# A layer kernel on one core: elementwise work of the mixer moved from GpSimd to VectorE, the tail's second factor and its half sums treated otherwise, and a new order list

## The chip, the cores and the metric

The kernel runs on one core of one Trainium2 chip. The metric is the device time of an execution in microseconds (us). The kernel before has a median of 1092.29 us over three timed runs (1090.87 to 1093.38). A difference of 0.2% is about 2.2 us here.

The engines are named as the profile names them: PE is TensorE (matmuls; PEld is its loading of weights), DVE is VectorE, ACT is ScalarE, POOL is GpSimd, SP is SyncE, which here only issues DMAs.

## The reference

One decoder layer over 512 tokens of width 1024, in float32. Two SwiGLU layers stand around a mixer, and a gated embedding follows. What the change touches is the second half of the mixer and the last norm.

```python
def swiglu(x, w_gate, w_up, w_down):
    return (jax.nn.silu(x @ w_gate) * (x @ w_up)) @ w_down

# mixer: proj = rmsnorm(h) @ w_in, split into u, v, z, xbc, dt_raw
ya = chunked_spatial_gating(gelu(u), gelu(v), ...)            # layernorm of v, product per head, * u
# Mamba-2 half, 2 groups of 8 heads of width 64, 4 chunks of 128 tokens:
xs, bm, cm = split(silu(causal_depthwise_conv(xbc)))
xdt = xs * dt
states = einsum(bm, xdt * decay_states)                       # per chunk
y = y_diag + y_off + xs * d_skip
y = y * silu(z)
y = y * rsqrt(mean(y * y, per group) + EPS) * norm_g
h = h + concatenate([rmsnorm(ya), y]) @ w_out

# tail
gate = sigmoid(rmsnorm(h) @ ple_w_gate + ple_b_gate)
h = h + gate * (p @ ple_w_proj)
return rmsnorm(h, final_norm)                                 # h * rsqrt(mean(h * h) + EPS) * g
```

## The kernel before, in words

Activations lie feature-major: eight tiles of 128 features by 512 tokens (`h`). Every matrix product is made of fp32r matmuls in three passes: a weight tile and an activation are each split into a rounded part and a rest (`whi`, `wlo`; `xhi`, `xlo`), and high*high, high*rest and rest*high are added in PSUM. Each weight tile of 128x1024 that arrives by DMA (`raw`, `rawb`, `rawd`, `r`) so costs one ACT copy (`whi<-raw`) and one DVE subtraction (`wlo<-raw,whi`).

The two SwiGLU layers and the mixer's products with `w_z`, `w_v`, `w_u` use a seven-product scheme on 2x2 blocks (`Group`, `Quads`). Some of its weight sums are made by DMAs that add into a tile; POOL issues these (`nc.gpsimd.dma_start(..., accum_op=ALU.add)`), SP issues the plain loads.

The program records all its operations, cuts them into numbered units, and issues the units in the order of a list, `ORDER`. Each engine then runs its own instructions strictly in that order, and semaphores hold an instruction back until its inputs are there. All of these instructions carry the line of the one place that issues them (L1896), so the profile is read by tile names.

The mixer, in the order of the program: the first projections and the causal convolution (`conv`: a DVE product `convin`, an ACT start, three DVE steps of 511, 510 and 509 columns into the tile `m` that becomes `xs[n]`, an ACT Silu); for each of the two groups of heads `gates(g)` (z by `Quads`), `ssd(g)` and `gated(g)`; then `values`, `spatial`, `outer`, `mix` for the other half, and the output product.

- `ssd(g)`: PE turns four `xs` tiles chunk by chunk (`b<-ident,m`), DVE multiplies by dt (`m<-b,dt`), POOL multiplies three of the four by the decay to the chunk's end (`m<-m,toend`), PE makes the states. Then for each of 8 heads ACT builds a decay tile `u`, DVE multiplies it (`u<-u,m`), and PE makes the products with `u`; DVE adds up `y` (`m<-m,vec,b` and `m<-m,m` of 384 columns).
- `gated(g)`: POOL multiplies four `xs` tiles by z (`m<-m,m` of 512 columns), ACT squares them, POOL adds the squares up (`ssum<-ssum,tmp`, three per group), PE sums over partitions (`b<-ones,ssum`), and DVE makes the factor and scales (`m<-m,vec,rall`).

The tail: the last three of the eight gate products are cut into two halves of 256 tokens. DVE adds each half's squares to `total` (the tile `ssum` of 512 columns); `factors` sums over partitions on PE and takes the root: for the first half by `rsqrt`, which is nine small DVE steps after two that start it, for the second by `rsqrt_by_table`, an ACT Sqrt with five small DVE steps. `rows_out` turns the eight `h` tiles (`b<-ident,h`), scales (`o<-b,rlast`, one tile in two on ACT, the other on DVE) and writes out.

Of the kernel before, what the change touches and what calls it, by code (L numbers as in the profile page):

```python
# [29 lines left out]
P = 128  # L30
T = 512
NC = T // P
D = 1024
# [43 lines left out]
for _name, _w in _VECS:  # L77
# [211 lines left out]
def layer_kernel(ctx: ExitStack, tc: tile.TileContext, a: dict, out: bass.AP):  # L289
# [1210 lines left out]
    def by_head(t):  # L1500
        return t.rearrange("p (h d) -> p h d", d=HD)

    group_norm = [Norm(), Norm()]
    yb = []

    def ssd(g):
# [82 lines left out]
    def gated(g, z):  # L1589
        for m in range(4):  # L1590
            y = xs[4 * g + m]
            nc.gpsimd.tensor_tensor(y, y, z[m], ALU.mult)
            group_norm[g].add(y)
# [410 lines left out]
```

## Time and profile before

| | before |
|---|---|
| median of three runs | 1092.29 us |
| profiled execution | 1095.35 us, of it the span from first to last instruction 1093.6 us |
| PE busy | 1072.8 us (98%), 7063 matmuls |
| DVE busy | 812.5 us (74%) |
| ACT busy | 550.8 us (50%) |
| POOL busy | 127.9 us (12%), 126 instructions |
| granted PE clock, mean | 0.994 |

A busy PE is not a PE at its peak, and the shares are means over stages with different limits. In rows of the timeline the first number is the start in us from the span's start, the second the duration in us; square brackets give the idle time of the engine before it and what ended it. In grouped rows stand the count, the busy time in us, the mean duration in ns, and the idle time before them. In rows by stage each engine has its busy us and its count of instructions; then come the granted clock of PE and the share of time that the DMA engines were busy.

### The profile page before, as it was taken

The page shows a single profiled execution, that of the slowest core. Times are in us where ns is not written, and L with a number is a line of the kernel's source. Part 1 is how long each engine was busy: PE and PEld are TensorE (multiplying, and loading weights), DVE is VectorE, ACT ScalarE, POOL GpSimd, SP SyncE. Part 2 cuts the span into 40 slices and gives each one's busy share as a digit, 9 for nine tenths or more (in the row PEclk, how much of TensorE's full clock was granted, in tenths as well). Part 3 has the DMA queues.
Part 4 walks back from the last instruction along what each step waited for, and adds up shares of the span by engine and source line. Part 5 has one row for each costly group of instructions (what it writes and reads, how often), then busy time and mean ns, then how long its engine had stood idle before and what let it go on. Part 6 is the DMA issues. An engine that isn't in the chain of part 4 may idle for free.

```text
span 1093.6 us, 17428 instructions
## 1 busy us (share of the span) xinstructions
PE 1072.8 (98%) x7063; PEld 966.2 (88%) x7063; DVE 812.5 (74%) x1139; ACT 550.8 (50%) x772; POOL 127.9 (12%) x126
## 2 busy tenths in 40 slices
PE   9999999999999999988999999999999999999996
PEld 7899999999998878887999878899999899999886
DVE  6887675757667789989989765778666675767748
ACT  7654353344345448767665434454444353443536
POOL 1100000000000400152610000000000000000110
PEclk9999999999999999989999999999999999999998
DMA  8968664775632344755766333667675665643412
GB/s 315 245 176 229 174 174 149 211 157 177 174 96 67 108 129 131 183 124 149 176 165 154 93 108 116 190 132 217 194 196 135 193 182 162 161 109 116 156 57 77
DMA packets 51633, 171.16 MB, mean 157 GB/s; under 512 B 5857, under 2 KB 6113, under 8 KB 51553
## 3 DMA queue, kind: packets, MB, share of 16 engines
q1 hardware_dynamic: 34128, 117.46, 31.4%
q0 software_dynamic: 11824, 43.00, 21.8%
q10 hardware_dynamic: 5600, 9.60, 2.8%
q8 instruction: 55, 0.90, 0.4%
q14 instruction: 26, 0.21, 0.1%
HBM read 165.77 MB, written 4.26 MB: 155 GB/s over the span
## 4 chain that ended last, share of the span: by engine, by line
PE 89%; DVE 5%; DMA 2%; issue 2%; ACT 1%; POOL 1%; DVEq 0%; SPq 0%; POOLq 0%; ACTq 0%
PE b L1896 73%; PE a L1896 16%; DVE m L1896 2%; DMA r<-in_w_z 2%; DVE wlo L1896 1%; DVE u L1896 1%; POOL m L1896 0%; DVE r L1896 0%; DMA g<-in_p 0%; ACT whi L1896 0%; ACT m L1896 0%; ACT L1896 0%; DVE tmp L1896 0%; POOL ssum L1896 0%; ACT u L1896 0%
## 5 line engine op out<-in xcount | busy, mean ns | idle before, releaser
L1896 PE MATMUL b<-xfb,whi 128*128 128x256 f32 (+1 forms) x1648 | 291.0, 280 | 0.0
L1896 PEld LDWEIGHTS b<-xfb,whi 128*128 128x128 f32 x1648 | 253.1, 188 | 6.9 <-issue 1.0
L1896 PE MATMUL b<-xfb,wlo 128*128 128x256 f32 (+1 forms) x824 | 230.7, 280 | 0.0
L1896 DVE TENSOR_TENSOR wlo<-raw,whi 128x1024 fp32r<-128x1024 f32 (+1 forms) x127 | 160.1, 1265 | 62.1 <-ACT whi L1896 60.0
L1896 ACT CAST whi<-raw 128x1024 fp32r<-128x1024 f32 (+1 forms) x128 | 133.2, 1042 | 124.6 <-PE b L1896 97.0
L1896 PEld LDWEIGHTS b<-xfb,wlo 128*128 128x128 f32 x824 | 154.7, 188 | 1.1
L1896 PE MATMUL b<-xfa,whi 128*128 128x256 f32 (+1 forms) x688 | 126.2, 285 | 0.0
L1896 PEld LDWEIGHTS b<-xfa,whi 128*128 128x128 f32 x688 | 106.4, 188 | 3.5
L1896 PE MATMUL b<-xfa,wlo 128*128 128x256 f32 (+1 forms) x344 | 98.1, 285 | 0.0
L1896 ACT CAST whix<-rawd 128x1024 fp32r<-128x1024 f32 (+1 forms) x40 | 39.5, 987 | 108.4 <-PE a L1896 58.4
L1896 ACT CAST whi<-rawb 128x1024 fp32r<-128x1024 f32 x52 | 54.6, 1049 | 65.8 <-PE b L1896 48.7
L1896 DVE TENSOR_TENSOR wlox<-rawd,whix 128x1024 fp32r<-128x1024 f32 (+1 forms) x40 | 45.6, 1141 | 43.5 <-ACT whix L1896 43.5
L1896 POOL DMA_DIRECT2D raw<-in_ffn_gu x30 | 33.2, 1125 | 360.1 <-DVE wlo L1896 165.6
L1896 DVE TENSOR_TENSOR wlo<-rawb,whi 128x1024 fp32r<-128x1024 f32 x52 | 63.5, 1221 | 13.9 <-ACT whi L1896 13.8
L1896 PE MATMUL b<-m,whi 128*128 128x512 f32 x224 | 70.7, 396 | 0.0
L1896 PEld LDWEIGHTS b<-xfa,wlo 128*128 128x128 f32 x344 | 64.6, 188 | 1.0
L1896 PE MATMUL b<-xb,whi 128*128 128x256 f32 (+1 forms) x280 | 63.4, 322 | 0.1
L1896 PE MATMUL b<-ghi,wlox 128*128 128x512 f32 x156 | 61.5, 394 | 0.0
L1896 PE MATMUL b<-glo,whix 128*128 128x512 f32 x156 | 61.3, 393 | 0.0
L1896 PE MATMUL b<-ghi,whix 128*128 128x512 f32 x156 | 60.7, 389 | 0.0
L1896 PE MATMUL a<-ghi,wlox 128*128 128x512 f32 x140 | 55.2, 394 | 0.0
L1896 PE MATMUL a<-glo,whix 128*128 128x512 f32 x140 | 54.9, 392 | 0.0
(295 smaller groups left out, 2305.7 us busy)
## 6 DMA issues: line engine op xcount, KB each, us to landing
raw<-in_ffn_gu SPq DMA_DIRECT2D x56, 512.0 KB, 5.4
rawd<-in_ffn_down SPq DMA_DIRECT2D x40, 512.0 KB, 5.2
rawb<-in_ffn_gu SPq DMA_DIRECT2D x32, 512.0 KB, 6.7
raw<-in_ffn_gu POOLq DMA_DIRECT2D x30, 512.0 KB, 7.9
s<-in_ffn_gu SPq DMA_DIRECT2D x20, 512.0 KB, 5.3
s<-in_ffn_gu POOLq DMA_DIRECT2D x20, 512.0 KB, 8.1
raw<-in_w_out SPq DMA_DIRECT2D x16, 512.0 KB, 3.7
raw<-in_w_in SPq DMA_DIRECT2D x13, 512.0 KB, 3.7
```

The source lines that it names most:

```text
L1896: getattr(getattr(real, engine), what)(*(real_of(x) for x in args), **{k: real_of(x) for k, x in kw.items()})
```

## The change

Five edits and a new list:

1. `group_norm = [Norm(), Norm()]` becomes `[Norm(nc.vector), Norm(nc.vector)]`: the three additions of squares per group, 128x512, go from POOL to DVE.
2. In `ssd`, the product with `to_end` (three per group, 128x512) goes from POOL to DVE.
3. In `gated`, the product with z (four per group, 128x512) goes from POOL to DVE. With these, 20 instructions of 128x512 move.
4. In the tail, the additions of the squares of the second and third last product (two per half, 128x256) go from DVE to POOL.
5. The first half's factor is taken by `rsqrt_by_table` too.
6. `ORDER` is made anew, in its first 240 units and from the middle of the mixer's first projections to the end of the output product, and in the last units.

```diff
@@ ssd, gated, and their norms
-    group_norm = [Norm(), Norm()]
+    group_norm = [Norm(nc.vector), Norm(nc.vector)]
...
                 xd = whole_m()
-                nc.gpsimd.tensor_tensor(by_head(xd), by_head(t), heads(to_end, g, c), ALU.mult)
+                nc.vector.tensor_tensor(by_head(xd), by_head(t), heads(to_end, g, c), ALU.mult)
...
             y = xs[4 * g + m]
-            nc.gpsimd.tensor_tensor(y, y, z[m], ALU.mult)
+            nc.vector.tensor_tensor(y, y, z[m], ALU.mult)
             group_norm[g].add(y)
@@ the tail: gate_half, factors
         if d < ND - 1:
-            nc.vector.tensor_tensor(total[:, tok], total[:, tok], sq, ALU.add)
+            nc.gpsimd.tensor_tensor(total[:, tok], total[:, tok], sq, ALU.add)
...
-        (rsqrt_by_table if tok.start else rsqrt)(rt, ps[:, :2], 1.0 / D, (P, 2))
+        rsqrt_by_table(rt, ps[:, :2], 1.0 / D, (P, 2))
@@ ORDER: one line of the list
-    "823 825 787 872 836 882 801-802 837 803 935 873 943 838 890 936 883 804 944-945 839-840 1015 841 805 "
+    "787 801-802 872 935 837 873 943 838 890 816 944 839-840 817 841-844 882 818 845-847 945 803 819 891 "
```

The list moves instructions at many places; three are shown.

**POOL, around `gated` of the second group.** Before (`m<-m,m` is the product with z, `ssum` the sum of squares, the DMAs add weight blocks):

```order
L1896 DMA raw_4984<-in_w_v 128x1024
L1896 TENSOR_TENSOR m_3773<-m_3773,m_4973 128x512
L1896 TENSOR_TENSOR m_3781<-m_3781,m_5157 128x512
L1896 TENSOR_TENSOR m_3776<-m_3776,m_5143 128x512
L1896 TENSOR_TENSOR m_4705<-m_4705,m_5160 128x512
L1896 TENSOR_TENSOR ssum_5306<-ssum_5306,tmp_5310 128x512
L1896 TENSOR_TENSOR ssum_5306<-ssum_5306,tmp_5322 128x512
L1896 TENSOR_TENSOR ssum_5306<-ssum_5306,tmp_5320 128x512
L1896 DMA r_797_5407<-in_w_v 128x1024
```

And after the change:

```order
L1896 DMA r_715_4861<-in_w_v 128x1024
L1896 DMA raw_5043<-in_w_v 128x1024
L1896 DMA r_787_5375<-in_w_v 128x1024
L1896 DMA raw_5379<-in_w_u 128x1024
L1896 DMA r_788_5377<-in_w_v 128x1024
```

Between the weight DMAs of the mixer POOL has no product and no sum left; two masks (`AFFINE_SELECT`) of the spatial part stay on it.

**DVE, ahead of the second group's turning.** The tile `m` whose three convolution steps (511, 510, 509) end last is the last one that PE turns. Before, the steps stand directly ahead of the first product with dt, which reads what PE turned:

```order
L1896 SCALAR_TENSOR_TENSOR m_4705<-convin_4585,vec_63,m_4705 128x511
L1896 TENSOR_TENSOR m_3774<-m_3774,m_3770 128x384
L1896 TENSOR_SCALAR nrt_121<-rtok_112 128x4
L1896 TENSOR_TENSOR wlo_4819<-r_662_4450,whi_4802 128x1024
L1896 TENSOR_TENSOR wlo_4821<-r_683_4607,whi_4806 128x1024
L1896 SCALAR_TENSOR_TENSOR m_4705<-convin_4585,vec_63,m_4705 128x510
L1896 SCALAR_TENSOR_TENSOR m_4705<-convin_4585,vec_63,m_4705 128x509
L1896 TENSOR_TENSOR wlo_4873<-raw_4611,whi_4812 128x1024
L1896 TENSOR_TENSOR m_4951<-b_4875,dt_122 128x512
```

After the change the last step of that convolution stands 37 rows ahead of that product; around the product:

```order
L1896 TENSOR_TENSOR r_663_4451<-r_663_4451,r_690_4638 128x1024
L1896 TENSOR_TENSOR wlo_4786<-r_690_4638,whi_4770 128x1024
L1896 TENSOR_TENSOR m_3870<-m_3870,m_3868 128x384
L1896 TENSOR_TENSOR wlo_4789<-r_663_4451,whi_4782 128x1024
L1896 TENSOR_TENSOR m_3870<-m_3870,m_4622 128x512
L1896 TENSOR_TENSOR m_3872<-m_3872,m_4540 128x512
L1896 TENSOR_TENSOR wlo_4890<-raw_4644,whi_4866 128x1024
L1896 TENSOR_TENSOR m_4892<-b_4793,dt_122 128x512
```

The two 512-column products with z (`m_3870`, `m_3872`), which were POOL's, stand there among the splits of weights.

**ACT, the tail.** `tmp<-tmp,vec` is a Sigmoid, `tmp<-h` a Square, `h<-h,vec` the last gain, `ny<-nv` the Sqrt. Before:

```order
L1896 ACTIVATE tmp_10758<-tmp_10758,vec_63 128x256
L1896 ACTIVATE h_96<-h_96,vec_63 128x512
L1896 ACTIVATE tmp_10771<-h_98 128x256
L1896 ACTIVATE h_98<-h_98,vec_63 128x256
L1896 ACTIVATE tmp_10774<-h_97 128x256
L1896 ACTIVATE h_97<-h_97,vec_63 128x256
L1896 ACTIVATE o_10427<-b_10800,rlast_141 128x512
L1896 ACT_TABLE_LOAD
L1896 ACTIVATE ny_10831<-nv_10826 128x2
```

After:

```order
L1896 ACTIVATE tmp_10762<-tmp_10762,vec_63 128x256
L1896 ACT_TABLE_LOAD
L1896 ACTIVATE ny_10769<-nv_10764 128x2
L1896 ACTIVATE tmp_10776<-h_95 128x256
L1896 ACTIVATE tmp_10778<-h_96 128x256
L1896 ACTIVATE o_10413<-b_10798,rlast_141 128x512
L1896 ACTIVATE o_10414<-b_10788,rlast_141 128x512
L1896 ACTIVATE h_95<-h_95,vec_63 128x256
L1896 ACTIVATE ny_10826<-nv_10821 128x2
```

The table load now stands ahead of the second half's two squares, and no load stands ahead of the second root.

233 rows, old and new, of the table ORDER are left out of this document.

## The prediction

> **What bounds the kernel now.** I read the page first, then PE's waits, then the mixer by stage.
>
> ```profile
> span 1093.6 us, 17428 instructions
> PE 1072.8 (98%) x7063; PEld 966.2 (88%) x7063; DVE 812.5 (74%) x1139; ACT 550.8 (50%) x772; POOL 127.9 (12%) x126
> ```
>
> PE is busy for all but 20.8 us of the span, and the change takes nothing off PE: its matmuls stay. So the time can fall only by idle PE time, by time at a lowered clock, and by what stands after the last matmuls. PE's waits in order of size:
>
> ```profile
> PE b L1896 <- ACT m L1896: 3.1, 1, 3.1
> PE b L1896 <- DVE m L1896: 2.1, 2, 1.1
> PE b L1896 <- DVE u L1896: 2.0, 2, 1.7
> ...
> PE b L1896 <- DVE ssum L1896: 1.3, 1, 1.3
> PE a L1896 <- DVE tmp L1896: 1.1, 1, 1.1
> PE a L1896 <- ACT a L1896: 0.7, 1, 0.7
> PE b L1896 <- DVE wlo L1896: 0.7, 1, 0.7
> PE a L1896 <- DVE wlo L1896: 0.7, 1, 0.7
> ```
>
> The columns are total, count, longest. The wait for `ssum` is the tail's; the other seven rows, 10.4 us in nine waits, lie in the mixer between 445 and 570 us. By stage:
>
> ```profile
> 10.00:45.00 35.00, 35.00 (x170) 28.93 (x169) 30.81 (x50) 23.66 (x35) 4.68 (x7) 1.00 0.91 307
> 427.00:532.00 105.00, 95.84 (x743) 87.43 (x741) 98.16 (x135) 77.69 (x143) 36.13 (x28) 0.97 0.64 162
> 483.00:491.00 8.00, 7.99 (x42) 8.00 (x43) 5.36 (x15) 4.88 (x14) 0.00 (x0) 0.57 0.63 149
> ```
>
> After the length stand PE, PEld, DVE, ACT, POOL, the granted clock, the DMA share. From 427 to 532 DVE is busy for 98.2 of 105 us, more than PE: there DVE sets the pace. And the third row shows a second loss, a granted clock of 0.57 over 8 us: 8 × 0.43 = 3.4 us of PE's work. It stands directly behind the largest gap:
>
> ```profile
> 478.80 3.43 DVE L1896 SCALAR_TENSOR_TENSOR m<-convin,vec,m 128x510 f32<-128x510 f32 x2
> 482.32 0.63 ACT L1896 ACTIVATE m<-m 128x512 f32<-128x512 f32 x1 [3.80 <-DVE m L1896]
> 483.01 1.39 PE L1896 MATMUL b<-ident,m 128*128 128x128 f32 x8 [3.12 <-ACT m L1896]
> ```
>
> PE's wait is put down to ACT's Silu, but ACT itself had waited 3.80 us for DVE: the last two convolution steps end late.
>
> **Why DVE is so full: POOL beside it.** The same instructions in the mixer's busy stretch (440 to 537 us), by form:
>
> ```profile
> L1896 DVE TENSOR_TENSOR wlo<-r,whi 128x1024 fp32r<-128x1024 f32 x14 | 20.9, 1496 | 0.3 <-ACT whi L1896 0.3
> L1896 DVE TENSOR_TENSOR u<-u,m 128x512 f32<-128x512 f32 x16 | 14.2, 909 | 0.0
> L1896 DVE TENSOR_TENSOR wlo<-raw,whi 128x1024 fp32r<-128x1024 f32 x5 | 9.9, 1987 | 0.0
> ...
> L1896 DVE TENSOR_TENSOR m<-m,m 128x384 f32<-128x384 f32 x8 | 5.8, 730 | 0.0
> L1896 DVE TENSOR_TENSOR m<-m,b 128x384 f32<-128x384 f32 x8 | 4.4, 550 | 0.0
> ...
> L1896 DVE SCALAR_TENSOR_TENSOR m<-convin,vec,m 128x511 f32<-128x511 f32 x2 | 2.5, 1262 | 0.0
> L1896 DVE SCALAR_TENSOR_TENSOR m<-convin,vec,m 128x510 f32<-128x510 f32 x2 | 2.5, 1254 | 0.0
> L1896 DVE SCALAR_TENSOR_TENSOR m<-convin,vec,m 128x509 f32<-128x509 f32 x2 | 2.4, 1186 | 0.0
> ```
>
> and behind the mixer, 580 to 700 us, where POOL computes nothing:
>
> ```profile
> L1896 DVE TENSOR_TENSOR wlo<-raw,whi 128x1024 fp32r<-128x1024 f32 x20 | 24.3, 1220 | 13.3 <-ACT whi L1896 11.3 <-PE b L1896 2.0
> ...
> L1896 DVE SCALAR_TENSOR_TENSOR m<-m,vec,rall 128x512 f32<-128x512 f32 x10 | 6.9, 744 | 0.0
> ...
> L1896 DVE TENSOR_TENSOR m<-m,tmp 128x512 f32<-128x512 f32 x8 | 5.4, 686 | 0.1
> ```
>
> The excess: 14 × (1496 − 1220) = 3.9; 16 × (909 − 686) = 3.6; 5 × (1987 − 1220) = 3.8; 8 × (730 − 550) = 1.4; the six convolution steps 2 × (1262 + 1254 + 1186 − 3 × 744) = 2.9. Together 15.6 us. The 384-column pair points at the cause: `m<-m,b`, with its second operand in PSUM, takes 550 ns, `m<-m,m`, both in SBUF, 730. What POOL does in the mixer:
>
> ```profile
> L1896 POOL TENSOR_TENSOR m<-m,m 128x512 f32<-128x512 f32 x8 | 14.9, 1883 | 6.7 <-DVE m L1896 4.1 <-ACT m L1896 2.1 <-issue 0.5
> L1896 POOL TENSOR_TENSOR ssum<-ssum,tmp 128x512 f32<-128x512 f32 x6 | 10.7, 1781 | 0.2
> L1896 POOL TENSOR_TENSOR m<-m,toend 128x512 f32<-128x512 f32 x6 | 6.8, 1318 | 1.6 <-DVE m L1896 1.6
> L1896 POOL DMA_DIRECT2D r<-in_w_z x4 | 3.5, 880 | 48.2 <-DVE wlo L1896 34.5 <-PE b L1896 13.8
> ```
>
> 20 instructions, 32.4 us. The Trainium skill ("GPSIMD Engine Reference", section "1. Specifications") says that GpSimd's path to SBUF is shared with VectorE, and that they contend where VectorE's instruction reads two inputs from SBUF; the 384-column pair (730 against 550 ns) agrees.
>
> **The change: the mixer.** *Added on DVE:* the 20 instructions. Such a one takes 0.68 us, and in a full queue the next begins after 0.60:
>
> ```profile
> 1071.43 0.68 DVE L1896 TENSOR_TENSOR h<-h,tmp 128x512 f32<-128x512 f32 x1
> 1072.03 0.68 DVE L1896 TENSOR_TENSOR tmp<-tmp,emb 128x512 f32<-128x512 f32 x1
> ```
>
> 20 × 0.60 = +12.0 us. *Relieved:* between 0 (the excess has another cause) and −15.6. I take −15.6, because the whole excess sits in instructions with two inputs in SBUF. DVE's balance there is −3.6 us. That is small; what counts is which waits end.
>
> *The 3.1 us gap.* In the new order the last convolution ends 37 DVE rows ahead of the product that reads its turned tile, so neither Silu nor turning is late: −3.1, and with it the 3.4 us at half clock behind it. The bounds for the clock are 0 (halved again behind another gap) and −3.4. I take −3.4, since the remaining gaps, of 1.7 us or less, left the clock whole everywhere else in the mixer: the mean of 0.97 over 105 us is those 3.4 us.
>
> *The 1.1 us gap* for `tmp` ends with its cause, DVE's wait for POOL's last sum:
>
> ```profile
> 531.74 0.69 DVE L1896 TENSOR_TENSOR tmp<-a,m 128x512 f32<-128x512 f32 x1 [1.18 <-POOL ssum L1896]
> ```
>
> On DVE the sum costs 0.60, counted above, and stands in DVE's own order: −1.1.
>
> *Given back.* A product with z on DVE now waits for the Silu of z with splits queued behind it; on POOL that was 2.1 us in all, seen in its row. So new waits cost between 0 and 2.1. I take +0.9, the mean of the seven mixer waits left (10.4 − 4.2 = 6.2 us). Mixer: −3.1 − 3.4 − 1.1 + 0.9 = **−6.7**. It fits DVE: 98.2 − 3.6 = 94.6 of 105 − 6.7 = 98.3 us is 96% busy, so little more can come. POOL's weight DMAs gain nothing from an empty POOL: they waited 34.5 us for `wlo`, a buffer still in use.
>
> **The change: the tail.**
>
> ```profile
> 1085.51 0.16 DVE L1896 TENSOR_SCALAR nv<-b 128x2 f32<-128x2 f32 x1
> ```
> ```profile
> 1081.23 0.71 ACT L1896 ACTIVATE h<-h,vec 128x512 f32<-128x512 f32 x1
> ...
> 1082.28 0.51 ACT L1896 ACTIVATE h<-h,vec 128x256 f32<-128x256 f32 x1
> ...
> 1085.24 1.28 ACT L1896 ACT_TABLE_LOAD   x1
> 1086.54 0.20 ACT L1896 ACTIVATE ny<-nv 128x2 f32<-128x2 f32 x1
> ```
>
> Before, the second root stood ready at 1085.67 and waited for the load until 1086.54: −0.87. Now load and first root (1.28 + 0.20) stand ahead of the second half's last squares, but two gains leave that place (0.71 + 0.51), so the squares end some 0.3 later. Then two sums on POOL replace two on DVE, there 0.34 each by half of the 512-column row of 0.68. No row has POOL at 256 columns; half of the means of its 512-column rows gives 0.66 to 0.94. One behind the other they cost 0.6 to 1.2 more. If the first runs under the next square, and since POOL's queue is empty where DVE's held the factor's steps between the sums, it may cost as little as nothing. Tail: −0.9 + 0.3 + (0 to 1.2) = −0.6 to +0.6. I take −0.3, nearer the low end, because the first sum needs only the first of the two squares. The new list's first 240 units I cost at 0 ± 0.3: from 10 to 45 us PE is busy without a break (first stage row), which covers a different order of splits there.
>
> The Trainium skill ("ScalarE: Activation LUTs", section "What ACT_TABLE_LOAD costs") adds a drain of 1.38 us to each load. By it the load ahead of the squares would make the tail 1.4 us worse, +1.1 in place of −0.3, and the sum 1086.7, still within the forecast's range. The trace disagrees: the load is one row of 1.28 us, and the root started 0.02 us after its end.
>
> **Sum.** −6.7 − 0.3 = −7.0. The profiled execution took 1095.35 us, 1.75 around its span; it would take 1088.3. It stood 3.1 over the median of the runs, so on their scale 1092.3 − 7.0 = **1085.3 us**.
>
> **Rivals.**
>
> *More.* Every mixer gap closes: −10.4 − 3.4 − 0.3 = −14.1, about 1078; with half of the rest, 1081.5, where I draw the line. For it: each remaining wait but one names DVE, and DVE gets faster. Against: DVE stays 96% busy. Chance 0.10.
>
> *No change.* The gaps only move. The accumulating DMAs take long beside a full DVE:
>
> ```profile
> 435.07 7.05 DMA r<-in_w_z
> ```
>
> If the new list puts the first use of such a transfer 4 us behind its issue, PE waits 3 us, the clock halves again behind that, and 3.1 + 3.4 come back: −0.5, about 1091.8. Against: the 14 splits that read `r` had only 0.3 us of idle time ahead of them (their row above). Chance 0.13.
>
> *Slower: DVE becomes the bound.* If the excess isn't POOL's but comes from DMA traffic, DVE must do 98.2 + 12.0 = 110.2 us in a stretch of 105: +5.2, about 1097.5. It decides if the relief falls below 12.0 − 6.8 = 5.2 of the 15.6 us (6.8 is DVE's idle time there). For it: DMAs are busy for 0.64 of these stages, and no run yet shows DVE there without POOL. Against: the 384-column pair, 730 and 550 ns, ran in the same stages beside the same transfers, and only the one with both operands in SBUF is slow; traffic alone would have to pick that one out too. Chance 0.15. The order leaves no doubt that POOL's mixer products are gone.
>
> **Numbers.** A measurement of this kernel tells 0.2%, 2.2 us, from no change, so faster begins at 1090.1. The forecast (1081.5 to 1090.1) has 0.62: its own terms (clock 0 to −3.4, new waits 0 to 2.1, tail and start to their ends) give 1083.8 to 1091.1. Faster: 0.62 + 0.10 = 0.72; same 0.13; slower 0.15. The range, 1079.5 to 1093.0, leaves out the slower case and the far end of "more".
>
> **What would show it.** The splits back at 1220 ns, `u<-u,m` at 686, and no DVE row near 2 us: the relief is POOL's. No halved stretch in the mixer, mean clock above 0.997, no PE wait for `ACT m` of 3 us: the large term holds. No DVE wait for POOL's `ssum` near 530 us; DVE's total near 812.5 − 3.6 = 809, a little below for the tail's four sums. In the tail: Sqrt directly behind its `nv`, and PE's wait for POOL's `ssum` near 1.3 us. Wrong is the forecast if `wlo` stays above 1.35 us without POOL, or if a new gap of 3 us or more appears; then the list, not the engine, decides.

## The result and the profile after

The change makes the kernel faster by more than was forecast: 1080.07 us (1079.39 to 1081.09, four runs) against 1092.84 us (1090.87 to 1095.73) for the kernel before. The ratio is 0.9882, its 95% interval 0.9858 to 0.9906, which is 10.3 to 15.5 us. The forecast was 1085.3 us with a range of 1079.5 to 1093.0. The measured time is in that range by 0.6 us only, and 1.4 us beyond the 1081.5 where the prediction drew the line to its rival "more".

The page of the kernel after, its first lines:

```profile
span 1077.7 us, 17409 instructions
PE 1067.5 (99%) x7063; PEld 962.3 (89%) x7063; DVE 803.8 (75%) x1149; ACT 550.1 (51%) x773; POOL 96.6 (9%) x110
```

PE now idles for 1077.7 − 1067.5 = 10.2 us of the span, where it was 20.8. The span is 15.9 us shorter: 10.6 of idle time, and 5.3 by which PE's own busy time shrank. (The medians differ by 12.8: the profiled execution of before stood 2.5 us over its median, that of after 0.7 under.)

The split of a weight tile that both kernels do near the end, and a sum that both do ahead of the mixer, show where the time went. The timeline of DVE, first before, then after:

```profile
342.32 0.68 DVE L1896 SCALAR_TENSOR_TENSOR h<-b,h 128x512 f32<-128x512 f32 x1
...
1058.26 1.23 DVE L1896 TENSOR_TENSOR wlo<-raw,whi 128x1024 fp32r<-128x1024 f32 x1 [0.19 <-ACT whi L1896]
```
```profile
341.87 0.68 DVE L1896 SCALAR_TENSOR_TENSOR h<-b,h 128x512 f32<-128x512 f32 x1
...
1041.39 1.23 DVE L1896 TENSOR_TENSOR wlo<-raw,whi 128x1024 fp32r<-128x1024 f32 x1 [0.19 <-ACT whi L1896]
```

Ahead of the mixer the kernel after is 0.4 us earlier, behind it 16.9: the stretch between gave 16.4, and since PE is busy without a break from 570 to 1040 us in both, that is the mixer. From that split to the end of the span it was 35.3 us and is now 36.3: the tail lost 1.0.

PE's waits after, all of them from 0.3 us up (total, count, longest):

```profile
PE b L1896 <- DVE tmp L1896: 1.7, 1, 1.7
PE b L1896 <- DVE h L1896: 1.2, 1, 1.2
PE b L1896 <- ACT whi L1896: 0.7, 1, 0.7
PE b L1896 <- ACT h L1896: 0.6, 1, 0.6
PE a L1896 <- ACT m L1896: 0.3, 1, 0.3
```

Only the last row lies in the mixer. The first and the third are the program's start, the two for `h` the tail. Of nine waits in the mixer, 10.4 us, one of 0.3 us is left. The stages of after, in the columns of the stage rows of before:

```profile
427.00:532.00 105.00, 105.00 (x877) 98.20 (x876) 101.36 (x160) 85.90 (x156) 11.53 (x14) 1.00 0.73 185
483.00:491.00 8.00, 8.00 (x68) 7.07 (x67) 7.47 (x22) 5.34 (x10) 0.00 (x0) 1.00 0.73 206
```

PE does not stand still once in these 105 us, the clock is whole, and DVE is fuller than before: 101.4 us, 97%. What DVE's instructions take there (425 to 520 us, by form):

```profile
L1896 DVE TENSOR_TENSOR wlo<-r,whi 128x1024 fp32r<-128x1024 f32 x15 | 18.3, 1218 | 0.8 <-ACT whi L1896 0.8
L1896 DVE TENSOR_TENSOR u<-u,m 128x512 f32<-128x512 f32 x16 | 10.8, 682 | 0.0
L1896 DVE TENSOR_TENSOR wlo<-raw,whi 128x1024 fp32r<-128x1024 f32 x7 | 8.5, 1214 | 0.0
...
L1896 DVE TENSOR_TENSOR m<-m,m 128x384 f32<-128x384 f32 x7 | 3.7, 548 | 0.0
```

1496, 909, 1987 and 730 ns have become 1218, 682, 1214 and 548, and the convolution steps take 740 ns in place of 1186 to 1262: the excess of 15.6 us is gone.

### The profile page after: what moved, and what is told of

The parts are those of the page before. It is cut to its first block, busy times and chain, and to the rows that moved or that the text cites. A ratio compares the mean times of both kernels' runs of the same rounds, so it can differ in the third digit from the quotient of the medians.

```text
span 1077.7 us, 17409 instructions
## 1 busy us (share of the span) xinstructions
PE 1067.5 (99%) x7063; PEld 962.3 (89%) x7063; DVE 803.8 (75%) x1149; ACT 550.1 (51%) x773; POOL 96.6 (9%) x110
## 4 chain that ended last, share of the span: by engine, by line
PE 98%; DVE 0%; ACT 0%; DMA 0%; issue 0%; DVEq 0%; SPq 0%; ACTq 0%
PE b L1896 80%; PE a L1896 18%; DMA raw<-in_ple_proj 0%; DVE o L1896 0%; ACT L1896 0%; DVE tmp L1896 0%; ACT tmp L1896 0%; DVE nt L1896 0%; ACT h L1896 0%; DVEq L1999 0%; ACT whi L1896 0%; ACT m L1896 0%; ACT ny L1896 0%; SPq L1896 0%; DVE h L1896 0%
## 5 line engine op out<-in xcount | busy, mean ns | idle before, releaser
L1896 DVE TENSOR_TENSOR wlo<-raw,whi 128x1024 fp32r<-128x1024 f32 (+1 forms) x127 | 155.2, 1228 | 51.2 <-ACT whi L1896 49.5
```

The costliest lines, as they stand in the source:

```text
L1896: getattr(getattr(real, engine), what)(*(real_of(x) for x in args), **{k: real_of(x) for k, x in kw.items()})
```

## The experiments

Three theories stood against each other. **A, sharing:** DVE's instructions with two operands in SBUF are slowed by POOL's work beside them, and with that gone DVE keeps up. **B, the list:** the new order is what closes the gaps. **C, POOL's queue:** results and DMA issues come late because they are queued behind other work on POOL. The kernel before, timed beside them, had medians of 1093.95 us (beside the first four kernels), 1093.58 (the second four) and 1094.31 (the last four).

| kernel | us | ratio to before, interval |
|---|---|---|
| moves, old list (`moves_old_list`) | 1091.06 | 0.9974 [0.9961, 0.9986] |
| new list, work on POOL (`new_list_pool`) | 1095.98 | 1.0018 [1.0007, 1.0030] |
| after, tail of before (`new_mixer_old_tail`) | 1079.76 | 0.9874 [0.9859, 0.9889] |
| after, 20 products more on DVE (`dve_fill`) | 1084.14 | 0.9916 [0.9901, 0.9931] |
| after, 36 products more on POOL (`pool_fill`) | 1089.39 | 0.9957 [0.9943, 0.9971] |
| `new_list_pool`, POOL's queue reordered (`pool_reordered`) | 1089.91 | 0.9965 [0.9946, 0.9985] |
| `moves_old_list`, three places mended (`moves_three_places`) | 1092.06 | 0.9984 [0.9972, 0.9996] |
| old list, the work on neither (`left_out_old_list`) | 1083.58 | 0.9904 [0.9888, 0.9920] |
| after, early table load (`early_load`) | 1078.57 | 0.9862 [0.9841, 0.9882] |
| after, half sums on DVE (`tail_sums_dve`) | 1079.84 | 0.9871 [0.9851, 0.9891] |
| after, again (`after_again`) | 1079.85 | 0.9870 [0.9846, 0.9893] |
| after, six sums on POOL (`sums_on_pool`) | 1089.77 | 0.9960 [0.9945, 0.9975] |

### Moves without the list, list without the moves

```diff
 the kernel before, ORDER unchanged (moves_old_list)
+    group_norm = [Norm(nc.vector), Norm(nc.vector)]
+                nc.vector.tensor_tensor(by_head(xd), by_head(t), heads(to_end, g, c), ALU.mult)
+            nc.vector.tensor_tensor(y, y, z[m], ALU.mult)
 the kernel after, ORDER unchanged (new_list_pool): the same three lines back to
+    group_norm = [Norm(), Norm()]; nc.gpsimd.tensor_tensor(...) in both
```

> The kernel before, with its own list and its own tail; only the 20 products and sums of the mixer go from GpSimd to VectorE. Theory A, the engine: what closes PE's gaps is that VectorE's instructions with two SBUF operands no longer share with GpSimd (15.6 us of excess gone for 12.0 us added). Then most of the gain is here too: 1081 to 1085 us against 1092 to 1093 before, the wait of PE for ACT m near 480 us falls from 3.1 to below 1 us, and wlo is back at 1.22 us. Theory B, the list: the old order still puts the last convolution directly ahead of the turning, and the moved products now stand in VectorE's queue at places chosen for another engine: 1088 to 1093 us, with a gap of 2 us or more left near 480 us though wlo is at 1.22 us.

> The changed kernel with its new list and new tail; only the 20 products and sums of the mixer go back to GpSimd. Theory A, the engine: VectorE gets the excess of about 15.6 us back and loses 12.0 us of work; with 101.4 of 105 us busy in the changed kernel it would be at 105 of 105, so waits come back: 1086 to 1092 us, wlo up to 2.3 us again. Theory B, the list: the earlier convolution and the work ahead hold even so: 1080 to 1084 us, with wlo slow but no gap over 1 us.

Neither half does it: 2.9 us faster with the moves alone, 2.0 slower with the list alone, 12.8 to 14.5 faster with both. Theory A's range for the moves (1081 to 1085 us) is missed, and both theories' ranges for the list alone. With the moves and the old list, PE's waits of 0.7 us and more, and then the stage, read:

```profile
PE b L1896 <- DVE tmp L1896: 3.9, 2, 2.3
PE b L1896 <- DVE m L1896: 2.0, 2, 1.5
PE a L1896 <- DVE tmp L1896: 1.6, 1, 1.6
PE b L1896 <- DVE ssum L1896: 1.3, 1, 1.3
PE a L1896 <- DVE wlo L1896: 1.0, 3, 0.4
PE a L1896 <- ACT a L1896: 0.7, 1, 0.7
```
```profile
427.00:532.00 105.00, 97.68 (x781) 89.65 (x780) 99.37 (x162) 79.32 (x144) 9.56 (x11) 0.98 0.66 170
```

The wait for `ACT m` has gone without any new order: with POOL's work gone from beside them, the convolution steps end early enough (0.2 us is left of 3.1). But other waits have come in its place, of 2.3, 1.5 and 1.6 us. For 97.7 us in which PE was busy DVE was busy for 99.4 here, 1.02 to one; in the kernel after it is 101.4 for 105.0, 0.97.

With the new list and the work on POOL, PE's two longest waits and the stage are others:

```profile
PE a L1896 <- ACT a L1896: 4.6, 1, 4.6
PE b L1896 <- POOL m L1896: 4.1, 1, 4.1
```
```profile
427.00:532.00 105.00, 99.95 (x801) 92.48 (x800) 90.46 (x135) 80.25 (x146) 36.00 (x28) 0.97 0.65 168
```

Over the stage DVE is not short of time, 90.5 of 105 us, where theory A expected 105: A's reason does not hold. Nor does sharing cost here what it cost before: `wlo<-r` takes 1410 ns and `wlo<-raw` 1575 (430 to 540 us), `u<-u,m` stays at 683. POOL's timeline shows the cause, with a row of DVE's behind it:

```profile
479.41 4.13 POOL L1896 TENSOR_TENSOR ssum<-ssum,tmp 128x512 f32<-128x512 f32 x2
483.51 1.05 POOL L1896 TENSOR_TENSOR m<-m,toend 128x512 f32<-128x512 f32 x1
...
521.42 5.24 POOL L1896 TENSOR_TENSOR m<-m,m 128x512 f32<-128x512 f32 x3 [8.89 <-DVE m L1896]
...
533.19 0.86 POOL L1896 DMA_DIRECT2D r<-in_w_v  x1
```
```profile
538.67 1.23 DVE L1896 TENSOR_TENSOR r<-r,r 128x1024 f32<-128x1024 f32 x1 [7.62 <-DMA r<-in_w_v]
```

The product with `to_end`, for which PE waits 4.1 us, stands behind two sums. And the DMA that adds a weight block is issued at 533.19, behind products and sums; DVE then waits 7.6 us for it and PE 4.6.

### POOL's queue

```diff
 POOL's order, new_list_pool -> pool_reordered
+L1896 TENSOR_TENSOR m_4894<-m_4892,toend_130 128x512
 L1896 TENSOR_TENSOR ssum_4870<-ssum_4870,tmp_4872 128x512
+L1896 TENSOR_TENSOR m_4899<-m_4897,toend_130 128x512
 L1896 TENSOR_TENSOR ssum_4870<-ssum_4870,tmp_4875 128x512
...
+L1896 DMA r_787_5375<-in_w_v 128x1024
+L1896 DMA raw_5379<-in_w_u 128x1024
 L1896 TENSOR_TENSOR ssum_5390<-ssum_5390,tmp_5388 128x512
```

> The new list with the 20 products and sums back on GpSimd (new_list_pool, 1096.0 us), and four instructions moved in GpSimd's queue: two products with to_end of the second group ahead of sums of squares, and the DMAs for r and raw that stood behind three products with z ahead of the sums and the fourth product. Theory C, GpSimd's queue: the two gaps of new_list_pool, 4.1 us (PE waits for a product with to_end that is queued behind sums) and 4.6 us (VectorE waits 7.6 us for a transfer whose issue is queued behind products), are made by the order in that queue, so both shrink below 1.5 us, and the half clock behind them goes: 1084 to 1089 us. Theory A, a full VectorE: the gaps only move, 1092 us or more.

It is between the two expectations: 6.1 us faster than `new_list_pool`, and the wait behind the transfer falls from 4.6 to 1.4 us. But the sums that stepped back are now late themselves; PE waits 4.5 us for one (in the execution that was traced, 1093.44 us):

```profile
PE b L1896 <- POOL ssum L1896: 5.2, 2, 4.5
...
PE a L1896 <- ACT a L1896: 1.4, 1, 1.4
```

So the queue's order sets which wait there is; this one order had no room for all three. Only the six sums of squares go back to POOL in the next kernel, all else as after:

```diff
-    group_norm = [Norm(nc.vector), Norm(nc.vector)]
+    group_norm = [Norm(), Norm()]
```

> The changed kernel with only the six sums of squares of the mixer back on GpSimd. VectorE is relieved of 3.6 us; GpSimd computes for 8 to 10 us beside it, which by the rate of before (15.6 us of excess for 32.4 us) gives some 4 to 5 us of excess. If VectorE's total decides, the two cancel: 1080 to 1082 us. If the sums on GpSimd come late for PE, as in pool_reordered (a gap of 4.5 us), a gap of 1 us or more stands ahead of the product with ones: 1082 to 1086 us.

This was missed by far: 9.9 us slower than the kernel after beside it (`after_again`), though the twelve DVE instructions beside those sums took only 1.0 us more than their clean durations (from their rows). The second group's sums in POOL's timeline, and what follows in DVE's:

```profile
520.42 1.99 POOL L1896 TENSOR_TENSOR ssum<-ssum,tmp 128x512 f32<-128x512 f32 x1 [12.73 <-ACT ssum L1896]
524.36 1.48 POOL L1896 TENSOR_TENSOR ssum<-ssum,tmp 128x512 f32<-128x512 f32 x1 [1.95 <-ACT tmp L1896]
525.78 0.85 POOL L1896 DMA_DIRECT2D r<-in_w_v  x1
```
```profile
532.33 1.23 DVE L1896 TENSOR_TENSOR r<-r,r 128x1024 f32<-128x1024 f32 x1 [5.94 <-DMA r<-in_w_v]
```

POOL waits 1.95 us for a square, the DMA issue stands behind that sum, DVE waits 5.9 us for the transfer, and PE 3.9 us in turn. The other group's sums cost a PE wait of 1.7 us. Behind each of the two the granted clock is lowered, to 0.81 over 9 us (482 to 491) and 0.84 over 11 us (535 to 546). Theory C holds: in this list an elementwise instruction on POOL delays what is queued behind it, the weights above all.

### How full DVE may be, and what sharing costs

```diff
 the kernel after, in the loop that issues the units
+            if n in range(1060, 1420, 18):    # pool_fill: range(1060, 1420, 10)
+                every_ident = ident.unsqueeze(1).to_broadcast([P, 2, P])
+                real.vector.tensor_tensor(    # pool_fill: real.gpsimd
+                    scratch.rearrange("p (c t) -> p c t", c=2), every_ident, every_ident, ALU.mult)
```

> The changed kernel with 20 products of 128x256 more on VectorE in the second half of the mixer, that nobody waits for: some 0.34 us each, 6.8 us in all. In the changed kernel VectorE is busy for 101.4 of 105 us (427 to 532) and PE doesn't wait there. If a VectorE this full is the bound, as the prediction's balance had it, 6.8 - 3.6 = 3.2 us or more come on top: 1083.3 us or more, with PE's waits for VectorE back. If the list has run far enough ahead that work can slip to the less busy stages behind, it is 1080 to 1081.5.

> The changed kernel with 36 products of 128x256 on GpSimd in the second half of the mixer, that nobody waits for and that touch no tile of the kernel but the constant ident. Clean they take about 0.77 us each (the tail's sums), some 28 us of GpSimd, as before the change (32.4 us there gave VectorE 15.6 us of excess). Theory A, sharing: VectorE's rows with two SBUF operands lengthen again, some 10 to 14 us in all, and since 6.8 us more on VectorE cost 4.1 us, this costs 7 to 11 us: 1087 to 1091 us. Rival: what cost time before was that results came late from GpSimd's queue, not the sharing: wlo stays near 1.22 us and the time at 1080 to 1081.5.

20 products of 0.34 us on DVE, 6.8 us, cost 4.1 us: DVE had about 2.7 us of room there. Beyond that it is the bound: PE idles for 2.9 of the 105 us from 427 to 532, and what it waits for there is DVE. The 36 on POOL, which touch nothing of the kernel's but a constant, cost 9.3 us. DVE's busy total rose by 9.6 us without one instruction more, POOL's products themselves taking 1066 ns each. The page, and the groups of DVE and of POOL by form (430 to 540 us; 35 of the 36 lie in it):

```profile
PE 1070.0 (98%) x7063; PEld 962.2 (89%) x7063; DVE 813.4 (75%) x1149; ACT 550.7 (51%) x773; POOL 132.5 (12%) x146
```
```profile
L1898 DVE TENSOR_TENSOR wlo<-r,whi 128x1024 fp32r<-128x1024 f32 x18 | 21.8, 1214 | 0.6 <-ACT whi L1898 0.6
L1898 DVE TENSOR_TENSOR u<-u,m 128x512 f32<-128x512 f32 x16 | 14.1, 885 | 0.0
```
```profile
L1915 POOL TENSOR_TENSOR scratch<-ident 128x256 bf16<-128x256 f32 x35 | 37.3, 1066 | 2.2
```

`u<-u,m` is at 885 ns, `wlo<-raw` at 1358, but `wlo<-r` stays clean at 1214. Which instructions lengthen depends on which run while POOL works: of the 18 `wlo<-r`, 15 had none of the 36 beside them. A mean by form hides this. In the kernel before, 15 of the 16 `u<-u,m` were clean, and one, beside three of POOL's products, made the whole excess:

```profile
501.29 4.27 DVE L1896 TENSOR_TENSOR u<-u,m 128x512 f32<-128x512 f32 x1
```
```profile
501.59 3.41 POOL L1896 TENSOR_TENSOR m<-m,toend 128x512 f32<-128x512 f32 x3
```

In `pool_fill` it is seven of the 16 that take 1.05 to 1.52 us. POOL's queue is no rival here: DVE's wait for a weight block that POOL's DMAs add is 0.9 us at most, as in the kernel after, and ACT's 2.5 (2.3 after). Sharing is shown. Its 9.6 us on DVE cost more of the kernel than the 2.7 us of room lead one to expect (6.9); the other 2.4 us are not explained.

### What the old list would do with more room

```diff
 the kernel before, ORDER unchanged but for the 20 units left out (left_out_old_list)
-                xd = whole_m()
-                nc.gpsimd.tensor_tensor(by_head(xd), by_head(t), heads(to_end, g, c), ALU.mult)
+                xd = t
-            nc.gpsimd.tensor_tensor(y, y, z[m], ALU.mult)
+    for norm in group_norm: norm.first_only = True    # sums of squares skipped
```
```diff
 moves_old_list, on DVE (moves_three_places):
   two weight splits behind   tmp<-ident,rtok   of the first group
   three   m<-m,toend   of the second group ahead of its products with u
   tmp<-a,m   ahead of the last two   ssum<-ssum,tmp
```

> The kernel before with its old list, and the 20 products and sums left out on both engines: the mixer's second half then lacks the products with z, the decay to the chunk's end and three of four squares per group in the sums. VectorE gets its 15.6 us back and nothing is added, GpSimd issues only DMAs. Theory A, VectorE short of time: with 82.6 of 105 us to do all its gaps go even by the old list, 1078 to 1082 us, and the new list is only needed to fit 12 us more in. If the old order by itself makes PE wait (a split ahead of what PE needs first), gaps of over 1 us are left: 1083 us or more.

> The old list with the moves (moves_old_list, 1091.1 us), and three places of VectorE's queue put right by hand, where its trace has PE's gaps of 2.3, 1.5 and 1.7 us: two weight splits behind the spread of the first group's factor, the products with to_end of the second group ahead of the decay products, and the product tmp ahead of the last sums of squares. If the new list is worth what these places are worth, the gaps fall to under 2 us in all and the time to 1083 to 1087 us. If VectorE is short of time as a whole there, other splits come late instead: 1088 to 1092 us, with the gaps at new places. The list's real part would then be what it moves out of the full stretch.

Without the work, and so with a POOL that only issues DMAs, the old list gives 1083.58 us: that is worth 10.0 us, and still 3.4 us of PE's waits stay in the mixer, though DVE is busy for only 94.3 us from 427 to 532:

```profile
PE b L1896 <- DVE m L1896: 1.9, 2, 1.4
...
PE a L1896 <- DVE wlo L1896: 0.8, 2, 0.7
PE a L1896 <- ACT a L1896: 0.7, 1, 0.7
```

With the 12 us of work back on DVE the old list is 7 us slower (1091.06). Mending the three places that wait doesn't help, 1092.06 us; two new waits for `u` take their place:

```profile
PE b L1896 <- DVE u L1896: 3.4, 2, 2.0
PE a L1896 <- DVE wlo L1896: 2.0, 4, 0.9
```

So this rearrangement of DVE's queue moves the waits and doesn't end them. One reading is that the old order asks too much of DVE in one stretch. The mixer can be cut by PE's own work in place of time, each instruction at the median of its form, 20 us of PE's work a piece. By this estimate the four fullest pieces hold some 85 us of DVE's work by the old list with the moves, for 80 us of PE, and some 81 by the new list; where the pieces begin and how overlaps are counted shifts both by 1 to 2 us. That this spreading is the list's part was not tried by itself, and it can't be the whole: with the work left out DVE had room, and 3.4 us of waits stayed.

### The tail

```diff
 new_mixer_old_tail: the kernel after with the tail's code and units of before
 tail_sums_dve: the kernel after with
+            nc.vector.tensor_tensor(total[:, tok], total[:, tok], sq, ALU.add)
 early_load: new_mixer_old_tail with, behind the last Square,
+                real.scalar.activation(vec_warm, ones[:, 0:1], AF.Sqrt)
   and the last gain behind the first output copy
```

> The changed kernel up to the tail, then the tail of before (half sums on VectorE, first factor by the small steps, its order). The trace of the changed kernel has its tail about 1.0 us longer than that of before, counted from the last common matmuls: the squares of the second half end 1.0 us later behind the table load, the two sums on GpSimd 1.0 us later. If that is the change's doing, this kernel ends 1.0 us earlier: 1079.1 us against 1080.1, and its tail has the length of before. If the later end came from elsewhere (a half clock in that one execution), it is 1080 or above.

> The changed kernel with the tail's four half sums back on VectorE; both factors still by the table. The two sums of the second half took 1.54 us on GpSimd one behind the other, on VectorE 0.34 each. If these sums are what made the second root 0.86 us later than before, the root comes 0.7 to 0.9 us earlier and the time is 1079.2 us. If it is the table load ahead of the squares, the root stays within 0.2 us of its place and the time at 1080.1.

> The changed kernel up to the tail, the tail of before, and in it the table load drawn ahead: a Sqrt of one column, whose result nobody reads, stands on ScalarE directly behind the last square, where ScalarE was idle for 0.90 us, and the last gain goes behind the first output copy. The second root then needn't wait for the load (0.87 us in the tail of before). If the load there hides in that idle time, the tail ends 0.8 us earlier than that of before and 1.7 us earlier than the changed one: 1078.4 us. If the load delays the output copies instead, 1079.2 or above.

> The changed kernel unaltered, for a comparison on the same chip: 1080.1 us, within 0.5.

The totals of the first two differ too little from the kernel after to be told apart. The traces tell them, counted from the split that was shown (before 1058.26, after 1041.39):

| | second Sqrt begins | end of span |
|---|---|---|
| before | 28.3 | 35.3 |
| after | 29.2 | 36.3 |
| after, again | 29.1 | 36.3 |
| tail of before | 28.3 | 35.4 |
| half sums on DVE | 29.0 | 36.2 |
| early load | 27.5 | 35.2 |

The new tail costs 1.0 us, and the old one gets them back. Putting the half sums back on DVE gains only 0.1. ACT after the change:

```profile
1064.59 0.49 ACT L1896 ACTIVATE tmp<-tmp,vec 128x256 f32<-128x256 f32 x1
1065.10 1.28 ACT L1896 ACT_TABLE_LOAD   x1
1066.39 0.20 ACT L1896 ACTIVATE ny<-nv 128x2 f32<-128x2 f32 x1
1066.50 0.71 ACT L1896 ACTIVATE tmp<-h 128x256 f32<-128x256 f32 x2
...
1070.54 0.20 ACT L1896 ACTIVATE ny<-nv 128x2 f32<-128x2 f32 x1 [0.87 <-DVE nv L1896]
```

The squares end 25.8 us behind the split where they ended at 24.8. Only 0.3 to 0.4 of that is the load ahead of them. The last sigmoid itself begins at 23.2 where it began at 22.6, since the three sigmoids of this half start late: DVE waits for PE ahead of the first, in the new order of the tail. And behind the squares the sum over partitions comes late on PE, which is still turning tiles:

```profile
1062.65 0.42 DVE L1896 TENSOR_TENSOR tmp<-b,rall 128x256 f32<-128x256 f32 x1 [0.84 <-PE b L1896]
```
```profile
1066.25 3.03 PE L1896 MATMUL b<-ident,h 128*128 128x128 f32 x13 [1.19 <-DVE h L1896]
1069.08 0.79 PE L1896 MATMUL b<-ones,ssum 128*128 128x1 f32 x4
```

POOL's half sums had ended at 1068.52, 0.6 us before PE took them; before the change PE had waited for them. With the sums on DVE they end 0.6 us earlier, but PE's turning is in the way all the same. So the sums on POOL were hidden behind PE, and the 1.0 us is the sum of these changes of order, less the 0.87 us that the second root no longer waits for its load.

With the load drawn into ACT's idle time the second root comes 0.8 us earlier than in the tail of before, as expected, but the end only 0.1 to 0.2: PE's last turning is in the way next, since ACT's copies wait 0.86 us for it. The median of 1078.57 us is the lowest of all and 1.3 us under the kernel after on the same chip, 0.12%, less than a comparison of these kernels can be sure of.

## Why the prediction was right, and where not

*Sharing.* Right in cause: the four rows are back at their clean durations, and `pool_fill` shows the sharing with POOL's DMAs no later than in the kernel after. The 15.6 us were right for the old list, but they are no fixed price of the 20 instructions: by the new list, back on POOL, they lengthened the weight splits by less and `u<-u,m` not at all. DVE's total fell to 803.8 us where about 809 was said; that rest was not taken apart. The rival that made DMA traffic the cause, and DVE the bound at 1097.5 us, fell with it: the DMA share in the stretch rose from 0.64 to 0.73 while the rows became clean.

*The 3.1 us gap and the clock.* Both went, −3.1 and −3.4 as said. The reason given was the earlier convolution. The moves alone leave 0.2 us of that gap, the list alone none: either was enough for this gap, though the list alone had the 4.1 us for POOL's product at the same turning. PE's busy total fell by 5.3 us between the two traces, 1.9 more than the 3.4; that rest was not taken apart either.

*The 1.1 us gap for POOL's last sum.* It went, but not because the sum is in DVE's order: with the old list the sums stood ahead of the same `tmp` on DVE, and PE waited 1.6 us.

*The step that failed* is "given back": seven mixer waits of 6.2 us were kept and 0.9 put on top, because DVE would be 96% busy, "so little more can come". DVE is 97% busy, and 0.3 us of waits is left. `dve_fill` confirms that DVE was near its limit; but a full engine makes nobody wait as long as each result comes before it is needed, and that is the doing of the list and the moves together. One of the kept waits was sharing itself: the longest, 1.7 us for `u`, stood behind the one `u<-u,m` of 4.27 us, and with the moves alone it is gone. The prediction had the excess as a mean over 16 and didn't see which wait it made. The list brought some 11 us against the old list with the same work (1080.07 against 1091.06). The balance was drawn over 105 us as if the work in them were fixed; by the new list both engines did more in the same 105 us (DVE 101.4 to PE's 105.0, where it was 98.2 to 95.8). The rival "more", 1078 us, described what happened, with a chance of 0.10. With 5.9 us of closed waits in place of the +0.9, and the tail's 1.0 in place of −0.3, the prediction's sum comes to 1079.8 us: two misses of opposite sign, of which the second hid a part of the first.

*POOL's DMAs.* That they gain nothing from an empty POOL was read from the old list, where they waited for a buffer. In the new list they stand behind POOL's work, and their delay is the larger of the two waits that cost 9.9 us for six sums. The mechanism named under "no change", a late transfer that adds a weight block, a 3 us wait and the clock behind it, is what `new_list_pool` and `sums_on_pool` show; an empty POOL is what keeps it out of the kernel after.

*The tail and the start.* For the tail −0.3 was said, +1.0 came. The 0.9 for the load was gained. The squares' delay, +0.3 from the durations on ACT's list, was 1.0: the load's part was 0.3 to 0.4 as said, but the sigmoids ahead of it were late too. The sums on POOL, allowed 0 to 1.2, cost 0.1. And a term is missing from the prediction: PE's turning ahead of the sum over partitions, some 0.6 us. The start gained 0.4 us, a little more than the 0.3 allowed.

The Trainium skill ("ScalarE: Activation LUTs", section "What ACT_TABLE_LOAD costs") had led to +1.1 by its drain of 1.38 us. That is near what was measured, but the trace disagrees with its reason: Sqrt begins 0.01 us behind the load's end here too.

## What to carry to other kernels

An engine's busy share says how much more work fits, not how much its users wait; to forecast a new order, look at each wait for the one instruction that makes it, not at means by form; the bottleneck engine's work per microsecond of the engine it feeds, piece by piece, is a guide that was not tested here by itself. Work on the engine that also issues DMAs has two prices, the slowing of its neighbour and the delay of every transfer queued behind it, and the second can be the larger. A move of work and the order made for it can each be worth little alone (here 2.9 us and −2.0, together some 13).

## What the runs showed of the hardware that was not expected

The time of the kernel before follows the granted clock: in its last twelve runs, 1091.2 to 1092.7 us at a mean of 0.996, 1094.1 to 1094.4 at 0.994, 1095.2 to 1095.4 at 0.993, 1096.4 at 0.991. Its sixteen runs beside the first four kernels follow it more loosely (1092.1 at 0.994, 1095.4 at 0.991). The kernel after, with next to no gap in the mixer, spread over 0.8 us in four runs (0.996 to 0.998) and over 1.7 in its first four. A reading that fits, though the kernel before has but one trace, is that a gap costs its length and then a slow stretch that differs from run to run. The one trace behind the prediction stood 3.1 us above the median of that kernel's first three runs.

Nor does the length of a gap decide whether the clock falls. Stages right behind a gap of 1.71 us in `sums_on_pool`, and behind one of 2.66 us in `pool_fill`:

```profile
483.00:487.00 4.00, 4.00 (x25) 4.00 (x25) 2.46 (x7) 3.55 (x7) 0.00 (x0) 0.63 0.50 101
```
```profile
457.00:463.00 6.00, 6.00 (x52) 6.00 (x53) 6.00 (x12) 3.82 (x10) 0.00 (x0) 1.00 0.20 58
```

The shorter gap was followed by a clock of 0.63, the longer by a whole one. The prediction's reason for a whole clock, remaining gaps of 1.7 us or less, was therefore no safe one.

The Trainium skill ("TensorE: Matmul & The Clock Gate", section "Part 1: The HAM clock gate (the "warmup" mystery)") has the clock set by windows of some 3.4 us that run freely and don't start anew with the kernel. A drop that does not go by a gap's length alone agrees with that; a drop behind a gap of half a window's length is more than its rule of one idle window gives.
